# DVE alone for the operations that DVE or POOL could do, after the attention of a two-layer streaming encoder

## The chip, the core and the metric

The program runs on one core of one Trainium2 chip. The core has a matrix engine (TensorE, PE in the profile; its weight loads are shown as PEld), three engines for elementwise work (VectorE or DVE, ScalarE or ACT, GpSimd or POOL) and SyncE (SP), whose queue issues the DMAs here. Each engine works through its own list of instructions in order, and semaphores hold an instruction until its inputs are there and its output buffer is free. The metric is the device time of one execution in microseconds; lower is better.

## What is computed

The reference is one inference step of two layers over a prompt of 2048 tokens and a sample of 32 tokens, width 1024, float32 throughout. Layer 0 projects, attends in two head groups (a sliding window and a chunk band), multiplies each head group's output with its SiLU gate and projects back. Layer 1 is a gated linear recurrence. Cut to what bears on the change:

```python
# layer 0, after the two attentions (oa, ob) and their gates (ga, gb)
y = jnp.concatenate([oa.reshape(b, t, -1) * jax.nn.silu(ga),
                     ob.reshape(b, t, -1) * jax.nn.silu(gb)], axis=-1)
m = y @ w_out
x = x + rms_norm(m, ln_post[0])
...
# layer 1
xb, z = jnp.split(rms_norm(x, ln_pre[1]) @ w_in, 2, axis=-1)
xp = jnp.concatenate([conv_state, xb], axis=1)
xc = conv_b + xp[:, 0:t] * conv_w[0]
for tap in range(1, CONV_W):
    xc = xc + xp[:, tap:tap + t] * conv_w[tap]
...
r = jax.nn.sigmoid(blockdiag(xc, wa) + ba)
gi = jax.nn.sigmoid(blockdiag(xc, wx) + bx)
log_a = C_GATE * r * jax.nn.log_sigmoid(lam)
a = jnp.exp(log_a)
u = jnp.sqrt(-jnp.expm1(2.0 * log_a)) * (gi * xc)
_, hs = lax.associative_scan(_lin_combine, (a, u), axis=1)
m = (hs * jax.nn.silu(z)) @ w_out
x = x + rms_norm(m, ln_post[1])
```

## The kernel before

**Tiling.** Activations lie transposed, channels on the 128 partitions and tokens along the free axis. The 2084 token columns (2048, four of padding, 32) are six blocks of 352 columns (the last 324); two blocks make one of three groups `b`. A float32 product is made of three faster ones: each operand is split into a high part and a remainder (`h = copy(x)` in a rounded type, `l = x - h`), and PE adds `wh*xh`, `wh*xl` and `wl*xh`. So every weight tile (128 x 1024) and every activation that PE reads needs one cast (ACT or DVE) and one subtraction (DVE or POOL). In the profile `wst` is the weight as loaded, `wh` and `wl` its parts, `r0h`, `r0l`, `r1h`, `r1l` the two sets of split activations.

**Stages.** First layer 0's input projections beside the attention; then, from `dense_2`, layer 0's out projections for the three groups (`out_part`), the first of which runs before the attention is over; then for each group layer 1's input projection (`in_part`) and out projection (`out_part`).

- `y_proc` makes the input of layer 0's out projections: product of attention output and gate (`xt<-xt`, `ex<-ex`), cast on ACT, subtraction (`r1l`, `r0l`).
- `out_part` runs the matmuls; for each finished accumulator `fin_out` scales it into `m` on ACT, squares it and adds the square to `sacc`; after the last of eight, the norm's factor `r` is made, and for each half block `m` is multiplied by `r` (`m<-m,r`) and the residual is added (`m<-m,xr` or with another buffer's name), each in a piece of five and one of three rows of 176 columns (128x880 and 128x528).
- `norm_proc` normalizes the next input and splits it.
- `in_part` has, for each of eight channel blocks, a convolution on DVE (`ex<-xb`), a split for the gate matmuls (`xs`), activations on ACT (`e`, `ti`, `a`), the recurrence as a scan on DVE, and the split of the result into the out projection's operand. The buffers `e` and `ti` are named `eti` and `ti` in the profile, `xc`, `a` and `sz` are `ex`. `gw_proc` loads and splits the gate weights (`gst`, `gh`, `gl`).
- `w_split` casts and subtracts each new weight tile. Of layer 1, weights are split once in group 0, stored, and loaded ready-split in groups 1 and 2.

**The order.** The program is written out by a list scheduler, `Sched`, when the kernel is built. Each piece of work is a generator that yields a request `Req`: its engine or engines, its inputs, its buffers and, where there are several engines, a cost for each. The scheduler keeps a model of when each engine and tile is free; `run` goes through the waiting requests by rank, and `pick` chooses the engine. An engine may be taken only when its modelled end lies at most `LOOK` (0.6 us for DVE and POOL) ahead of the current time; among several, the one that ends first is taken. Ranks: 0 for `fin_out` and its additions, 0.4 for the convolution's chain, 0.5 for `y_proc`, 3 for `w_split`, which goes to 0.5 when no split weight is in hand. Requests that name DVE and POOL are those for `wl`, `r0l`/`r1l`, `xt<-xt`, `sacc`, `ss`, `m`, `xs`, `gl` and one product on `ti`. Others name DVE and ACT (the casts) or one engine alone. The loop over the engines of a request, with the line numbers of the profile's kernel:

```python
329        for i, e in enumerate(req.eng):
330            if e == "PE":
331                if t <= self.now + EPSR / 2:
332                    best = (0, e)
333                continue
334            if self.t[e] > self.now + LOOK[e] or t > max(self.now, self.t[e]) + EPSR:
335                continue
336            f = max(self.t[e], t) + (req.cost[i] if req.cost else 0.0) + (VPEN if e == "V" else 0.0)
```

All instructions go through the one helper at line 101, so the profile shows L101 for nearly every one of them; tiles are told apart by name.

Of the kernel before, what the change touches and what calls it, by code (L numbers as in the profile page):

```python
# [83 lines left out]
class Eng:  # L84


    def __init__(self, sch, name, eng):
        self.sch, self.name, self.eng = sch, name, eng
# [77 lines left out]
class Sched:  # L166
# [3 lines left out]
    def __init__(self):  # L170
        self.t = {"PE": 0.0, "A": 0.0, "V": 0.0, "G": 0.0, "SP": 0.0, "DMA": 0.0}
        self.w, self.r, self.key = {}, {}, {}
        self.procs = []
        self.now = 0.0
        self.n = 0
        self.tab = None
        self.lock = {"V": [], "G": []}
        self.win, self.busy, self.half = 0, 0.0, False
        self.pem, self.vpt = PEMA, VPTA
        self.halves, self.cuts, self.loaded = set(), {}, set()  # L180
# [100 lines left out]
    def set(self, key, t=None):  # L281
        self.key[key] = self.now if t is None else t

    def spawn(self, gen, prio):
        self.n += 1
        p = [prio, self.n, gen, None]
        p[3] = next(gen, None)
        if p[3] is not None:
            self.procs.append(p)
            self.procs.sort(key=lambda q: (q[0], q[1]))  # L290
# [30 lines left out]
    def pick(self, req):  # L321

        t = self.avail(req)
        if t is None:
            return None
        if req.eng[0] == "SP" and req.ins and not isinstance(req.ins[0], tuple):
            t += SPM
        best = None
        for i, e in enumerate(req.eng):
            if e == "PE":  # L330
                if t <= self.now + EPSR / 2:
                    best = (0, e)
                continue
            if self.t[e] > self.now + LOOK[e] or t > max(self.now, self.t[e]) + EPSR:
                continue
            f = max(self.t[e], t) + (req.cost[i] if req.cost else 0.0) + (VPEN if e == "V" else 0.0)
            if best is None or f < best[0]:
                best = (f, e)
        if best and req.func and self.tab and req.func != self.tab:

            if req.since is None:
                req.since = self.now
            if self.now < req.since + 1.0:
                return None
        return best and best[1]
# [49 lines left out]
def hybrid_kernel(ctx, tc, I, O):  # L395
    nc = tc.nc
    sch = Sched()
    V, A, G, PE, SP = [Eng(sch, n, e) for n, e in (("V", nc.vector), ("A", nc.scalar), ("G", nc.gpsimd),
                                                  ("PE", nc.tensor), ("SP", nc.sync))]
# [380 lines left out]
    def y_proc(b, ri, key, free=None, then=None):  # L780

        hh, hl = RT[ri]
        todo = [(bi, t0, col, w, 4 * j) for bi, t0, col, w in cells_of(b) for j in range(2)]
        cur = {}

        def y_load():
            for n, (_, t0, _, w, k0) in enumerate(todo):
                g = xrr if b == 0 and n % 3 == 2 else xtr
                x, = yield R("SP", [("o", min(b + 1, 2)), ("z", b)], [g])
                for j, src in enumerate((oT, zT)):  # L790
                    SP.dma_start(out=x[:, 4 * j:4 * j + 4, :w],
                                 in_=src[k0 * 128:k0 * 128 + 512, t0:t0 + w].rearrange("(k p) t -> p k t", p=128))
                cur[n] = x, g
                sch.set((key, "x", n))
        spawn(y_load(), PY if b == 0 else PY2)
        for n, (bi, t0, col, w, k0) in enumerate(todo):
            yield R("V", [(key, "x", n)])
            x, g = cur[n]
            o = x[:, 0:4, :w]
            e, _ = yield R(("V", "G"), [x], cost=(0.8, 1.63))  # L800
            ENG[e].tensor_tensor(o, o, x[:, 4:8, :w], OP.mult)
            ks, cs = slice(k0, k0 + 4), slice(col, col + w)
            yield R("A", [x] + ([(free, bi)] if free else []))
            A.copy(hh[:, ks, cs], o)
            th = sch.t["A"] + 0.13
            e, _ = yield R(("V", "G"), [lambda: th], cost=(0.8, 1.63))
            ENG[e].tensor_tensor(hl[:, ks, cs], o, f32(hh[:, ks, cs]), OP.subtract)
            g.release(x)
            if n % 4 == 3:
                sch.set((key, bi), max(sch.t["V"], sch.t["G"]) + 0.13)  # L810
        if then:
            then()
# [974 lines left out]
    def gw_proc():  # L1787

        for b in range(3):
            for c in range(8):  # L1790
                g, = yield R("SP", rings=[gstr])
                SP.dma_start(out=g, in_=I["gw"][c])
                e, (gh, gl) = yield R(("A", "V"), [g], [ghr, glr], cost=(0.3, 0.2))
                if e == "A":
                    A.copy(gh, g)
                else:
                    V.tensor_copy(gh, g)
                e, _ = yield R(("V", "G"), [gh], cost=(0.33, 0.69))
                ENG[e].tensor_tensor(gl, g, f32(gh), OP.subtract)
                gws[(b, c)] = gh, gl  # L1800
                gstr.release(g)
                sch.set(("gw", b, c), sch.t[e] + 0.13)
# [147 lines left out]
    def dense_2():  # L1950
        for b in range(3):
            yield from out_part(b, base + 8 * b, b % 2, I["xT"], LN_POST, x2T, lambda k, bi, b=b: (("y", b), bi), late_m=b > 0)
            if b == 0:

                yield R("PE", [("attention",)])
        spawn(gw_proc(), 1)
        xrr.retire(eti)
        for x in extra:
            xtr.retire(x)
        b1 = base + 24  # L1960
        for b in range(3):
            yield from in_part(b, b1 + 24 * b, 1, 0)
            if b < 2:
                spawn(norm_proc(x2T, b + 1, LN_PRE + 1, 1, (1, b + 1), [xtr, xtr], free=("in", b), src_ready=[("x2", b + 1)]), PY3)
            yield from out_part(b, b1 + 24 * b + 16, 0, x2T, LN_POST + 1, O["yT"], lambda k, bi, b=b: ("yc", b, k), late=True, final=b == 2)

    spawn(dense_2(), 9)
    sch.run(lambda: not names() & {"kq_proc", "v_proc", "proc", "reduce"})
    P.close()
# [25 lines left out]
    ar, szr = [Ring(sch, None, None, None, t, 1, tiles=[x]) for t, x in zip(("a", "sz"), parts[1])]  # L1995
    xtr.idle += [(0.0, -1, x) for x in extra]
    sch.set(("attention",))
    sch.pem, sch.vpt = PEM, VPT
    spawn(y_proc(1, 1, ("y", 1), then=y2), PY2)
    sch.run(lambda: not sch.procs)  # L2000
# [114 lines left out]
```

## Time and profile before

| what | us |
| --- | --- |
| median of three runs | 1881.93 |
| lowest and highest of them | 1880.21, 1882.59 |
| the profiled execution's own time | 1876.91 |
| its span in the profile | 1875.1 |

The profile is of one execution. Busy times are summed per engine and can lie beside each other; a matmul's time overlaps with the next one's. A row of a timeline gives start, duration, engine, line, operation, output and inputs with their shapes, and in brackets the idle time of the engine before it and what ended that. Where rows have "wait" in mind, as in "PE acc <- POOL wl", the engine on the left stood idle, and the instruction on the right was the one it waited for last. The stretches are in microseconds from the span's start.

### The profile page before, as it was taken

How to read it: one execution, taken by the hardware profiler on the slowest of the kernel's cores; microseconds unless marked ns; L12 is line 12 of the kernel's file. 1: busy time of each engine (PE TensorE's matmuls, PEld its weight loads, DVE VectorE, ACT ScalarE, POOL GpSimd, SP SyncE). 2: the span in 40 equal slices, each digit the busy share in tenths (PEclk: the TensorE clock that was granted, in tenths of full speed). 3: DMA queues.
4: the chain of work that ended last, by engine and by line, in shares of the span. 5: the costliest groups of instructions: out<-in, count | busy, mean ns of one | idle time of the engine just before them, and what ended most of it. 6: DMA issues, size and time to landing. Idle time of an engine off the chain costs nothing. (4 is left out here: it accounts for less than half of the span.)

```text
span 1875.1 us, 31799 instructions
## 1 busy us (share of the span) xinstructions
PE 1743.0 (93%) x11078; PEld 1686.8 (90%) x11078; DVE 1590.4 (85%) x3168; ACT 1002.5 (53%) x2048; POOL 610.6 (33%) x433
## 2 busy tenths in 40 slices
PE   8999999999999999999989969989889999999995
PEld 7999999889899999999979959988889999998995
DVE  8999967999999679989897879799898988699943
ACT  4276632476657337656564343456663586447831
POOL 4332214322223232221242646654423320153112
PEclk8999999999999999999999979999889999999997
DMA  5798856887554487877765884585455834565376
GB/s 177 205 252 262 233 151 211 228 249 211 168 157 119 128 237 186 245 202 203 212 190 153 225 231 134 191 258 175 154 174 186 238 121 149 182 200 167 128 269 177
DMA packets 293577, 362.80 MB, mean 193 GB/s; under 512 B 36309, under 2 KB 244617, under 8 KB 293401
## 3 DMA queue, kind: packets, MB, share of 16 engines
q1 hardware_dynamic: 293416, 360.78, 65.3%
q8 instruction: 87, 1.43, 0.3%
q14 instruction: 74, 0.60, 0.1%
HBM read 255.77 MB, written 107.00 MB: 193 GB/s over the span
## 5 line engine op out<-in xcount | busy, mean ns | idle before, releaser
L101 PE MATMUL acc<-r0h,wh 128*128 128x352 f32 (+2 forms) x1832 | 594.6, 325 | 16.3 <-ACT r0h L101 6.6
L101 PE MATMUL acc<-r0l,wh 128*128 128x352 f32 (+2 forms) x1832 | 595.1, 325 | 1.3 <-DVE r0l L101 1.3
L101 PE MATMUL acc<-r0h,wl 128*128 128x352 f32 (+2 forms) x1832 | 594.4, 324 | 1.5 <-DMA wl<-wo1s 1.5
L101 PEld LDWEIGHTS acc<-r0h,wh 128*128 128x128 f32 x1832 | 348.3, 190 | 19.4 <-ACT r0h L101 7.2
L101 PEld LDWEIGHTS acc<-r0l,wh 128*128 128x128 f32 x1832 | 348.2, 190 | 3.2 <-DVE r0l L101 2.2
L101 PEld LDWEIGHTS acc<-r0h,wl 128*128 128x128 f32 x1832 | 348.2, 190 | 3.2 <-DMA wl<-wo1s 2.5
L101 PE MATMUL acc<-r1h,wh 128*128 128x352 f32 (+1 forms) x864 | 282.8, 327 | 22.4 <-ACT xb L101 14.1
L101 PE MATMUL acc<-r1h,wl 128*128 128x352 f32 (+1 forms) x864 | 281.1, 325 | 15.2 <-POOL wl L101 15.2
L101 PE MATMUL acc<-r1l,wh 128*128 128x352 f32 (+1 forms) x864 | 281.0, 325 | 0.0
L101 POOL TENSOR_SCALAR pt<-pt,rr 128x256 f32<-128x256 f32 (+4 forms) x142 | 100.0, 715 | 366.2 <-DVE rr L101 214.3
L101 POOL TENSOR_TENSOR wl<-wst,wh 128x1024 fp32r<-128x1024 f32 x62 | 155.6, 2509 | 186.3 <-ACT wh L101 109.3
L101 ACT ACTIVATE pt<-pt,nm 128x256 f32<-128x256 f32 (+6 forms) x272 | 169.7, 626 | 61.2 <-DVE nm L101 59.3
L101 PEld LDWEIGHTS acc<-r1h,wh 128*128 128x128 f32 x864 | 166.1, 192 | 25.4 <-ACT xb L101 16.1
L101 PEld LDWEIGHTS acc<-r1h,wl 128*128 128x128 f32 x864 | 165.8, 192 | 15.5 <-POOL wl L101 15.5
L101 ACT CAST pp<-T 128x256 fp32r<-128x256 f32 (+4 forms) x314 | 134.0, 438 | 84.7 <-PE T L101 66.0
L101 PEld LDWEIGHTS acc<-r1l,wh 128*128 128x128 f32 x864 | 166.2, 192 | 0.0
L101 PE MATMUL T<-ident,pt 128*128 128x128 f32 (+2 forms) x864 | 143.4, 274 | 18.3 <-DVE pp L101 10.3
L101 DVE TENSOR_TENSOR pp<-T,pp 128x256 fp32r<-128x256 f32 (+4 forms) x314 | 150.4, 496 | 7.8 <-ACT pp L101 6.0
L101 PE MATMUL O<-pp,vt 128*128 128x256 f32 (+3 forms) x728 | 135.8, 309 | 10.0 <-DVE pp L101 4.7
L101 PEld LDWEIGHTS T<-ident,pt 128*128 128x128 f32 (+2 forms) x864 | 101.7, 140 | 42.7 <-DVE pp L101 19.9
L101 ACT CAST wh<-wst 128x1024 fp32r<-128x1024 f32 x70 | 73.5, 1049 | 99.7 <-PE acc L101 72.9
L101 PE MATMUL S<-kk,qa 128*128 128x320 f32 (+5 forms) x376 | 120.3, 334 | 3.6 <-issue 1.6
(252 smaller groups left out, 3312.8 us busy)
## 6 DMA issues: line engine op xcount, KB each, us to landing
wst<-w_in SPq DMA_DIRECT2D x93, 512.0 KB, 4.3
wst<-wo_in SPq DMA_DIRECT2D x32, 512.0 KB, 4.4
wh<-w1s SPq DMA_DIRECT2D x32, 512.0 KB, 3.7
wl<-w1s SPq DMA_DIRECT2D x32, 512.0 KB, 4.6
wh<-wo1s SPq DMA_DIRECT2D x24, 512.0 KB, 3.8
wl<-wo1s SPq DMA_DIRECT2D x24, 512.0 KB, 4.6
kk<-kB SPq DMA_DIRECT2D x32, 320.0 KB, 4.9
vt<-vB SPq DMA_DIRECT2D x16, 640.0 KB, 4.8
```

What stands on the lines that cost most here:

```text
L101: r = fn(*a, **k)
```

## The change

The scheduler gets a switch, `alone`. While it is on, `pick` passes over POOL for every request that names more than one engine; requests for POOL alone, and those for DVE and ACT, are as before. It is switched on when the attention's work is all placed, off after each input projection of layer 1 is placed, and on again ahead of the next one; after the last input projection it stays off. Nothing else is edited; the order of all later instructions is worked out anew by the scheduler.

```diff
@@ -175,6 +175,8 @@
         self.lock = {"V": [], "G": []}
+
+        self.alone = False
@@ -330,6 +332,8 @@
             if e == "PE":
                 if t <= self.now + EPSR / 2:
                     best = (0, e)
+                continue
+            if e == "G" and len(req.eng) > 1 and self.alone:
                 continue
@@ -1959,7 +1963,9 @@
         for b in range(3):
+            sch.alone = True
             yield from in_part(b, b1 + 24 * b, 1, 0)
+            sch.alone = False
             if b < 2:
                 spawn(norm_proc(x2T, b + 1, LN_PRE + 1, 1, (1, b + 1), [xtr, xtr], free=("in", b), src_ready=[("x2", b + 1)]), PY3)
@@ -1995,6 +2001,7 @@
     sch.set(("attention",))
+    sch.alone = True
     sch.pem, sch.vpt = PEM, VPT
```

## Prediction

> **What bounds the kernel now.** I read the page's busy times first, then TensorE's waits, then the busy time of each engine by stage, and last the timelines of DVE and POOL beside each other.
>
> ```profile
> span 1875.1 us, 31799 instructions
> PE 1743.0 (93%) x11078; PEld 1686.8 (90%) x11078; DVE 1590.4 (85%) x3168; ACT 1002.5 (53%) x2048; POOL 610.6 (33%) x433
> ```
>
> TensorE (PE) bounds the whole, but the share is a mean over stages. The windows cut the part that the change can touch into its stages; their columns are the stretch, its length, then busy time of PE, PEld, DVE, ACT and POOL, PE's granted clock, DMA share and GB/s.
>
> ```profile
> 1008.00:1206.00 198.00, 172.38 (x1051) 170.23 (x1050) 160.60 (x151) 75.59 (x136) 113.97 (x58) 0.94 0.71 204
> 1206.00:1364.00 158.00, 140.95 (x833) 138.90 (x832) 145.90 (x146) 97.00 (x128) 80.77 (x39) 0.95 0.60 200
> 1364.00:1442.00 78.00, 68.51 (x393) 66.72 (x392) 65.63 (x86) 38.60 (x60) 16.33 (x10) 0.91 0.53 180
> 1442.00:1586.00 144.00, 137.17 (x841) 135.38 (x840) 128.81 (x159) 94.83 (x124) 39.85 (x23) 0.99 0.52 160
> 1586.00:1649.00 63.00, 62.13 (x386) 61.35 (x385) 45.25 (x68) 28.12 (x50) 7.91 (x6) 1.00 0.59 189
> 1649.00:1786.00 137.00, 131.54 (x841) 129.54 (x840) 129.22 (x182) 96.28 (x155) 45.94 (x26) 1.00 0.55 166
> 1786.00:1875.00 89.00, 66.10 (x418) 63.86 (x416) 33.59 (x37) 19.33 (x41) 18.21 (x9) 0.89 0.74 228
> ```
>
> In order: the rest of layer 0's out projections, then layer 1's input and out projections in turn for the three token groups. The three input projections give PE nearly the same matmuls, and the first takes 158 us where the last takes 137. In the first DVE is busy 145.9 of 158 us. So the first two stages lose PE time, and DVE is full or nearly full. PE's waits over these stages (total, times, longest):
>
> ```profile
> PE acc L101 <- POOL wl L101: 15.2, 1, 15.2
> PE acc L101 <- ACT xb L101: 14.1, 6, 4.9
> PE acc L101 <- DVE ex L101: 8.3, 3, 4.7
> PE acc L101 <- ACT r0h L101: 6.6, 2, 5.7
> PE g L101 <- DVE xs L101: 6.4, 7, 1.6
> PE misc L101 <- DVE xs L101: 6.1, 2, 5.8
> PE acc L101 <- ACT tz L101: 3.2, 2, 2.2
> ```
>
> These seven come to 59.9 us, nearly all that can be won. `xb` on ACT waits for its one buffer, which DVE's convolution on `ex` frees, and `r0h` follows DVE's chain on `ti`; so most of the 59.9 us is DVE or POOL being late. Is DVE late by its own work? Its timeline beside POOL's:
>
> ```profile
> 1042.48 0.89 DVE L101 TENSOR_TENSOR r1l<-xt,r1h 128x704 fp32r<-128x704 f32 x1 [2.41 <-ACT r1h L101]
> ...
> 1046.27 3.14 DVE L101 TENSOR_TENSOR r1l<-xt,r1h 128x704 fp32r<-128x704 f32 x1 [0.24 <-ACT r1h L101]
> ```
>
> ```profile
> 1046.26 2.41 POOL L101 TENSOR_TENSOR wl<-wst,wh 128x1024 fp32r<-128x1024 f32 x1 [4.62 <-DVE wh L101]
> ```
>
> The same subtraction takes 0.89 us with POOL idle and 3.14 us when a POOL op of 2.41 us starts with it: 2.41 + 0.73. DVE stood still until POOL was done. The columns here are start, duration, engine, and the rest as named. A smaller tile even takes longer than a larger one:
>
> ```profile
> 1208.98 1.07 DVE L101 TENSOR_TENSOR m<-m,r 128x880 f32<-128x880 f32 x1
> ...
> 1211.52 2.59 DVE L101 TENSOR_TENSOR m<-m,r 128x528 f32<-128x528 f32 x1
> ```
>
> [...]
>
> **The change, part by part.** It adds no instruction, DMA or semaphore of its own; it takes POOL out of the choice for every request that names two engines, from the end of the attention on except while an out projection of layer 1 runs. The attention's last DVE op in the trace:
>
> ```profile
> 1007.96 0.42 DVE L101 TENSOR_TENSOR ot<-ot 64x256 f32<-64x256 f32 x1
> ```
>
> The first 1008 us are planned as before, and I count nothing there, nor in the two later out projections' own stretches or after 1786 us.
>
> *What goes onto DVE.* Prices of the same forms, first POOL's groups over all stages (count, busy us, mean ns), then DVE's ops with POOL idle:
>
> ```profile
> L101 POOL TENSOR_TENSOR wl<-wst,wh 128x1024 fp32r<-128x1024 f32 x24 | 63.2, 2634 | 62.1 <-ACT wh L101 30.1 <-DVE wh L101 15.7 <-PE g L101 9.0
> L101 POOL TENSOR_TENSOR xs<-ex,xs 64x704 fp32r<-64x704 f32 x12 | 25.7, 2140 | 18.1 <-DVE xs L101 10.3 <-ACT xs L101 7.6
> L101 POOL TENSOR_TENSOR m<-m,r 128x880 f32<-128x880 f32 x9 | 22.9, 2549 | 4.6 <-DVE r L101 4.3
> ```
>
> ```profile
> 1235.10 1.80 DVE L101 TENSOR_TENSOR xs<-ex,xs 64x704 fp32r<-64x704 f32 x2
> ...
> 1251.59 1.21 DVE L101 TENSOR_TENSOR wl<-wst,wh 128x1024 fp32r<-128x1024 f32 x1
> ```
>
> `wl` is 2.634 / 1.21 = 2.18, `xs` 2.140 / 0.90 = 2.38, `m` 2.549 / 1.07 = 2.38; I use 2.3. POOL's busy time in the four stages then costs DVE 113.97 / 2.3 = 49.6, 80.77 / 2.3 = 35.1, 39.85 / 2.3 = 17.3 and 45.94 / 2.3 = 20.0 us.
>
> *What goes from DVE.* I went through DVE's timeline of each stage, op by op, and took from each op the median of the same form with no POOL op beside it (for `m` 128x528, which never ran so, 0.67 us, an estimate scaled from the 1.07 us of 128x880). Ops over by more than 0.3 us were 38, 32, 19 and 22; first and last of each stage:
>
> ```profile
> 1014.39 1.64 DVE L101 TENSOR_TENSOR ex<-ex 128x704 f32<-128x704 f32 x1
> ...
> 1198.32 1.27 DVE L101 CAST wh<-wst 128x1024 fp32r<-128x1024 f32 x1 [3.44 <-PE acc L101]
> ...
> 1359.99 2.29 DVE L101 SCALAR_TENSOR_TENSOR ex<-xb,vec,ex 128x704 f32<-128x704 f32 x1
> ...
> 1442.62 2.41 DVE L101 TENSOR_TENSOR r1l<-xt,r1h 128x704 fp32r<-128x704 f32 x1
> ...
> 1575.67 1.43 DVE L101 TENSOR_TENSOR eti<-eti 128x704 f32<-128x704 f32 x1
> ...
> 1649.82 1.66 DVE L101 TENSOR_TENSOR xs<-sacc,xs 128x352 fp32r<-128x352 f32 x1
> ...
> 1777.13 2.32 DVE L101 SCALAR_TENSOR_TENSOR eti<-ex,eti 128x676 f32<-128x676 f32 x1
> ```
>
> (The second stage's first is the 2.59 us row above.) Their excess sums to 58.0, 46.9, 20.0 and 24.5 us. Net, DVE's load goes from 160.6 to 152.2, from 145.9 to 134.1, from 128.8 to 126.1 and from 129.2 to 124.7 us: 8.4 + 11.8 + 2.7 + 4.5 = 27.4 us less in all, though DVE does everything. In addition each moved op is ready in under half the time.
>
> *First stage, -8 us.* Its largest stall is one weight:
>
> ```profile
> 1090.57 0.66 PE L101 MATMUL acc<-r1h,wl 128*128 128x352 f32 x1 [15.21 <-POOL wl L101]
> ```
>
> ```profile
> 1055.00:1091.00 36.00, 20.52 (x125) 19.94 (x124) 31.73 (x19) 10.03 (x16) 29.48 (x14) 0.84 0.74 186
> ```
>
> In these 36 us POOL works 29.5 us ahead of and on that `wl`, and 17.2 us of DVE's 31.7 are such excess (same count). On DVE alone: 31.7 - 17.2 + 29.5 / 2.3 = 27.3 us, some 4.4 us less busy; with a part of the gaps between, 6 us off the 15.2. Next late is the 5.8 us wait for `xs` and the weight after it; with them -8, about the stage's net load.
>
> *First input projection, -9 us.* At 92% DVE sets the pace, so most of its 11.8 us should come back; I take three quarters, as the chain of PE, ACT and DVE of one column block has latency of its own.
>
> *Second and third, -2.5 and -2.5 us*: little PE time is lost there (144 and 137 us against 158).
>
> *The end of the first input projection, -2 us*: the 5.7 us wait for `r0h` follows DVE's last chain.
>
> Sum -24 us. The profiled execution took 1876.91 us (span 1875.1), so 1852.9 us; it lies 5.0 us under the median of the three runs, 1881.93, to which I apply the sum: **1858 us**.
>
> *Bounds.* If the excess stayed, each stage would take POOL's price less DVE's free time: 49.6 - 37.4, 35.1 - 12.1, 17.3 - 15.2 and 20.0 - 7.8, together +49.5 us. At the other end, all seven waits gone is -59.9 us. I stand nearer the second, since 3.14 = 2.41 + 0.73 is a row of this very stage.
>
> *Costed at nothing:* DVE's in-order queue. A `wl` or `gl` that had POOL to itself now stands among `m`, `xs` and the convolution, and whatever is behind it on DVE waits 0.4 to 1.2 us; SP's stores of `m` and PE's weights come behind that. It is covered as long as DVE's load stays under the stage; in the first input projection that cover is 158 - 134.1 = 24 us.
>
> **The rivals.**
>
> *Weights come late (slower).* The planner ranks weight splits last until no spare weight is in hand, and DVE is then the only engine for the subtraction. 24 `wl` were POOL's. If half of them were late by the running op (about 1), the own 1.2 us and the rest of a burst of `m` (about 1), that is 12 x 3.2 = 38 us; less the 17 us of the first two stages, and without the later 7, +21: 1903 us. It decides once `m`, `y` and the convolution alone keep DVE over about nine tenths. For it: 134.1 / 158 is 85% with bursts; against it: the worst weight now is late because of POOL.
>
> *DVE's order eats the gain.* Loads fall, but the new order puts other waits in place of the old ones: 0 to -9 us, about 1877 us. For it: the waits by `xb` and `xs` are the chain's, not POOL's alone.
>
> *DVE full.* [...] As a mechanism here: DVE's stretched time is real work, the price adds up, +49.5: 1931 us. The 0.89 and 3.14 us rows speak against it.
>
> *It does not do what it says*: the switch is set as the order is written, so the last `m` of an out projection may still be placed under the next input projection. That moves some 12 ops of 1 us, nothing that decides.
>
> **How the numbers follow.** The forecast (-10 to -46 us) 0.55, beyond that 0.03; eaten gain 0.20, half of it within 0.2%; late weights 0.17; DVE full 0.04; not as said 0.01, counted as no change. 0.2% is 3.8 us, about what a measurement can tell from no change. Faster 0.55 + 0.03 + 0.10 = 0.68, same 0.11, slower 0.21. The range 1836 to 1890 takes in the forecast, the eaten gain and the mild end of late weights.
>
> **What the next profile would show.** Right: POOL near zero from 1008 us but for the out projections; no `m` 128x528 on DVE over 0.8 us; the 15.2 us wait for `wl` under 10; the first input projection some 150 us. Wrong: PE waiting for DVE's `wl` again and again (late weights), or DVE above 97% with ops at their short durations (DVE full).

## The result and the profile after

| kernel | median us | lowest to highest |
| --- | --- | --- |
| before | 1882.26 | 1880.21 to 1882.73 |
| after | 1823.38 | 1822.28 to 1829.82 |

The ratio is 0.9696, with a 95% interval of 0.9673 to 0.972: 58.9 us less. The direction was right, and the size was not: 24 us were forecast, and the time lies below the range, which began at 1836. The profiled execution after took 1823.5 us, 53.4 us less than the one before, and its span is 53.4 us shorter too. The page of after:

```profile
span 1821.7 us, 31694 instructions
...
PE 1731.5 (95%) x11078; PEld 1671.8 (92%) x11078; DVE 1555.3 (85%) x3330; ACT 996.5 (55%) x2037; POOL 326.5 (18%) x284
```

DVE runs 162 instructions more than before and is busy 35.1 us less. PE's 11078 matmuls take 11.5 us less; the other 41.9 us of the span are idle time of PE that is gone. The windows of after, cut at the first matmul of each stage (columns as in the prediction: stretch, length, busy PE, PEld, DVE, ACT and POOL, granted clock, DMA share, GB/s):

```profile
1008.00:1183.30 175.30, 166.68 (x1039) 164.99 (x1038) 147.25 (x207) 76.70 (x135) 0.00 (x0) 0.99 0.80 233
1183.30:1327.60 144.30, 136.26 (x837) 132.82 (x836) 140.33 (x201) 101.85 (x131) 0.00 (x0) 1.00 0.59 202
1327.60:1393.30 65.70, 64.14 (x390) 63.52 (x390) 57.87 (x81) 30.42 (x50) 12.69 (x8) 0.97 0.69 238
1393.30:1537.00 143.70, 137.11 (x837) 133.24 (x836) 126.33 (x185) 92.24 (x120) 1.01 (x1) 1.00 0.52 160
1537.00:1600.50 63.50, 62.69 (x391) 61.90 (x390) 45.49 (x69) 28.45 (x50) 8.05 (x6) 1.00 0.58 188
1600.50:1735.50 135.00, 132.72 (x837) 130.06 (x837) 122.27 (x210) 93.80 (x152) 0.00 (x0) 1.00 0.54 168
1735.50:1821.70 86.20, 65.22 (x420) 62.61 (x418) 34.19 (x38) 19.47 (x41) 16.73 (x8) 0.92 0.73 236
```

POOL is at zero in the first and second stage and in the last input projection; its 1.0 us in the second input projection are the tail of an operation begun in the out projection. The granted clock of the first three stages rises from 0.94, 0.95 and 0.91 to 0.99, 1.00 and 0.97. Lengths by the same cut, in us ("same_order" is the first experiment below; L0 is the rest of layer 0's out projections, in and out are layer 1's projections of groups 0, 1, 2):

```
             L0    in0    out0   in1    out1   in2    last
before      198.0  157.3   78.8  143.4   63.7  136.6   89.3
after       175.3  144.3   65.7  143.7   63.5  135.0   86.2
difference  -22.7  -13.0  -13.1   +0.3   -0.2   -1.6   -3.1   sum -53.4
same_order  196.0  145.8   78.3  141.1   63.5  130.2   89.1   (sum -23.1 to before)
```

48.8 of the 53.4 us come from the first three stages. The cut at 1008 us also takes in what was won or lost earlier, where none of these three kernels is changed and PE's list is the same. The last matmuls of the attention show it (before, after, same_order):

```profile
1002.89 1.35 PE L101 MATMUL O<-pp,vt 128*128 128x256 f32 x10
...
1000.95 1.35 PE L101 MATMUL O<-pp,vt 128*128 128x256 f32 x10
...
1008.99 1.35 PE L101 MATMUL O<-pp,vt 128*128 128x256 f32 x10
```

So 1.9 us of the change's 53.4 lie ahead of it, and same_order comes 6.1 us late into its first stage; why single executions differ there isn't shown. Counted from these rows to the end of the span, the change gains 51.5 us and same_order 29.2. The rest of layer 0's out projections then takes 203.1 us before, 182.3 after and 195.0 in same_order.

PE's waits after, from 1000 us to the end (total, times, longest):

```profile
PE g L101 <- DVE xs L101: 11.0, 14, 2.8
PE acc L101 <- ACT tz L101: 3.6, 3, 2.1
PE acc L101 <- DMA wl<-wo1s: 2.9, 4, 1.1
PE acc L101 <- ACT tzb L101: 2.9, 1, 2.9
...
PE acc L101 <- DVE wl L101: 1.6, 1, 1.6
```

The 15.2 us for `wl`, the 14.1 for `xb` and the 6.6 for `r0h` are gone. What is left is short: no wait is over 2.9 us.

### The profile page after: what moved, and what is told of

The parts are those of the page before. It is cut to its first block, busy times and chain, and to the rows that moved or that the text cites. A ratio compares the mean times of both kernels' runs of the same rounds, so it can differ in the third digit from the quotient of the medians.

```text
span 1821.7 us, 31694 instructions
## 1 busy us (share of the span) xinstructions
PE 1731.5 (95%) x11078; PEld 1671.8 (92%) x11078; DVE 1555.3 (85%) x3330; ACT 996.5 (55%) x2037; POOL 326.5 (18%) x284
## 4 chain that ended last, share of the span: by engine, by line
PE 49%; DVE 29%; DMA 9%; ACT 6%; issue 4%; SPq 1%; POOL 1%; DVEq 0%; ACTq 0%; POOLq 0%
PE acc L101 35%; PE T L101 4%; PE O L101 4%; PE S L101 4%; DVE pt L101 3%; DVE ex L101 3%; DVE m L101 3%; DMA xr<-x2T 3%; DVE ss L101 2%; DVE ti L101 2%; DVE xs L101 2%; DVE s L101 2%; DVE pp L101 2%; DVE eti L101 1%; DVE wl L101 1%
## 5 line engine op out<-in xcount | busy, mean ns | idle before, releaser
L101 PE MATMUL acc<-r1h,wh 128*128 128x352 f32 (+1 forms) x864 | 277.5, 321 | 5.2 <-ACT tz L101 3.6
L101 PE MATMUL acc<-r1h,wl 128*128 128x352 f32 (+1 forms) x864 | 277.0, 321 | 1.6 <-DVE wl L101 1.6
L101 PE MATMUL acc<-r1l,wh 128*128 128x352 f32 (+1 forms) x864 | 276.9, 321 | 0.0
L101 PEld LDWEIGHTS acc<-r1h,wh 128*128 128x128 f32 x864 | 162.3, 188 | 6.4 <-ACT tz L101 4.5
L101 PEld LDWEIGHTS acc<-r1l,wh 128*128 128x128 f32 x864 | 162.3, 188 | 0.0
L101 DVE CUSTOM_DVE_ANT_0 pt<-S,bias 128x320 f32<-128x320 f32 (+2 forms) x240 | 108.8, 478 | 17.4 <-PE S L101 14.6
L101 PEld LDWEIGHTS O<-pp,vt 128*128 128x128 f32 (+1 forms) x728 | 107.1, 193 | 16.0 <-DVE pp L101 6.1
```

Source lines behind the costliest of these rows:

```text
L101: r = fn(*a, **k)
```

## The experiments

Two theories stand against each other. **Standstill**: the gain is DVE no longer stopping behind POOL, and the order of the instructions is a side effect. **Order**: with one fast engine in place of two, the scheduler writes another order for every engine (and shares the casts out anew between DVE and ACT), and that order is a gain of its own. Ratios are to the kernel before on the same chip, whose median lay between 1870.84 and 1877.28 us; intervals are of 95%.

### same_order: before's order, POOL's operations on DVE

The scheduler plans as before; each operation that it gives to POOL from the attention's end on, where the change would bar POOL, is written into DVE's list at that place. The lists of PE, ACT and SP stay as they were.

```diff
-        fn = getattr(self.eng, op)
+        fn = getattr(self.sch.dve if self.name == "G" and self.sch.alone else self.eng, op)
...
-            if e == "G" and len(req.eng) > 1 and self.alone:
-                continue
```

> The order of before kept for PE, ACT and SP, and 142 instructions moved from POOL into DVE's list where the planner had put them; nothing is planned anew. Theory P (DVE stands still while POOL works, and every queue that waits for either is late): most of the 58.9 us comes back without a new plan, 1825 to 1845 us, and the 15.2 us wait of PE for wl falls under 6. Rival O (the gain is the new order: the weight's cast moved ahead of the m block in ACT's list): the time stays at 1865 us or more, since ACT's list is that of before and the cast still stands behind the m block.

Measured: 1854.13 us against 1876.37, ratio 0.9873 (0.9843 to 0.9902): 22.2 us less of the 58.9, between the times that the two theories gave. By the traces 146 instructions have moved (POOL has 433 before and 287 here). The groups of DVE by form, from 1008 to 1790 us, show that the standstills are gone. First before, then same_order (count | busy us, mean ns | idle before):

```profile
L101 DVE TENSOR_TENSOR m<-m,r 128x528 f32<-128x528 f32 x9 | 23.1, 2569 | 0.0
...
L101 DVE COPY hist<-xb 128x3 f32<-128x3 f32 x24 | 10.0, 415 | 0.4
```

```profile
L101 DVE TENSOR_TENSOR m<-m,r 128x528 f32<-128x528 f32 x18 | 12.6, 700 | 0.0
...
L101 DVE COPY hist<-xb 128x3 f32<-128x3 f32 x24 | 3.9, 164 | 0.8 <-ACT xb L101 0.3
```

DVE does twice as many of these `m` in about half the time. The windows of same_order, its first three stages:

```profile
1008.00:1204.00 196.00, 177.58 (x1093) 175.59 (x1092) 152.28 (x213) 77.67 (x140) 0.94 (x1) 0.96 0.71 205
1204.00:1349.80 145.80, 135.83 (x828) 134.40 (x828) 132.17 (x185) 96.34 (x127) 0.00 (x0) 0.98 0.66 216
1349.80:1428.10 78.30, 67.84 (x398) 66.10 (x397) 65.69 (x86) 39.07 (x61) 15.17 (x10) 0.93 0.54 180
```

The first input projection has the gain, 11.5 us, and so has the first stage once it is counted from the attention's last matmuls, 8.1 us; the first out projection has nearly none. PE's waits, from 1008 to 1800 us:

```profile
PE acc L101 <- DVE wl L101: 9.3, 1, 9.3
PE misc L101 <- DVE xs L101: 9.1, 5, 5.3
PE acc L101 <- ACT r0h L101: 7.9, 2, 5.7
```

The longest wait falls from 15.2 to 9.3 us and stays at its place; the 5.7 us for `r0h` at the start of the first out projection do not move at all. So the standstills are worth 22 us under the old order by the medians, and 29 by the profiles from the attention's end; the rest of the 58.9 us is not theirs.

### l0_only and in_only: the switch in one part each

```diff
@@ l0_only, ahead of each in_part
-            sch.alone = True
+            sch.alone = False
@@ in_only, at the end of the attention
-    sch.alone = True
```

> DVE alone only from the end of the attention to the first input projection of layer 1; POOL is used again after that. Theory P: the first stage shortens by some 22 us as in the changed kernel (198 to 175 us) and the later stages stay as before: 1857 to 1862 us. Rival S (the stages are not independent, a good start of the input projection needs the first one too): under 1850 us.

> DVE alone only in the three input projections of layer 1; the rest of layer 0's out projections keeps POOL. Theory P: the first input projection and the out projection behind it shorten by 13 us each, the others by 2 or 3 together: 1850 to 1860 us, and with the other half this sums to the 58.9 us. If the first stage's gain carries the rest: over 1868 us.

Measured: l0_only 1857.0 us, ratio 0.9891 (0.986 to 0.9922); in_only 1867.86 us, 0.9945 (0.9928 to 0.9962). Their gains, 19.4 and 8.5 us, are 27.9 together, some half of what the whole gives. l0_only's first stage is 177.6 us, 2.3 longer than the change's; counted from the attention's last matmuls the two are alike (182.6 and 182.3 us). in_only gains in its first input and out projections (145.2 and 63.0 us) and loses it in the second input projection, at 161.6 us; there PE's waits show one large one:

```profile
PE acc L101 <- ACT r1h L101: 16.4, 1, 16.4
```

Nothing in POOL's absence explains a new wait of 16.4 us: each variant has an order of its own, and they do not add up. in_only's time lies in neither of the ranges given for it, just under the 1868 us of the rival.

### wl_only: POOL left out for the weights alone

```diff
-            if e == "G" and len(req.eng) > 1 and self.alone:
+            if e == "G" and len(req.eng) > 1 and self.alone and req.cost == (1.14, 2.3):
```

> Only the weights' subtraction wl leaves POOL, 24 of its groups' instructions, 63 of about 280 us of POOL time in the four stages; everything else may use POOL as before. If the gain is the weight that PE waited 15.2 us for: 1855 us or less. Theory P (each us of POOL costs DVE nearly as much, whatever the operation): about 63/280 of 58.9 us, so 1865 to 1872 us.

Measured: 1864.01 us, 0.9933 (0.9906 to 0.9959). This is the rival of late weights where it does occur:

```profile
PE acc L101 <- DVE wl L101: 35.9, 3, 17.1
```

With POOL still at `m`, `xs` and the rest, a weight on DVE queues behind operations that stand still. The timeline has it ahead of the two longest: at the 17.1 us a `sacc` takes 2.35 us (0.57 on average in same_order) and the weight itself 2.58 for 1.21, and at the 13.2 us four pieces of `xt` take 5.56 us together (0.52 each in same_order) beside POOL's `r1l`. In the changed kernel the same wait is 1.6 us.

### after_pool and no_lock: the new order with POOL in it, and a plan without the lock

after_pool keeps the lists of PE, ACT and SP of the changed kernel and gives every second of the operations concerned to POOL (163 were counted ahead of the run; the traces have 166, POOL going from 284 to 450). no_lock lets POOL in, and takes out the scheduler's model of DVE and POOL shutting each other out (`book` moves an operation behind a running one of the other engine where all operands lie in SBUF).

```diff
@@ after_pool, where every second request of a cost sets ghost
-        fn = getattr(self.eng, op)
+        fn = getattr(self.sch.gps if self.name == "V" and self.sch.ghost else self.eng, op)
@@ no_lock, in book (the skip in pick goes too, and so does the switching off)
-        if e in ("V", "G") and op not in ("reciprocal", "tensor_reduce") and all(str(x.space).endswith("SB") for x in outs + ins):
+        if not self.alone and e in ("V", "G") and op not in ("reciprocal", "tensor_reduce") and all(str(x.space).endswith("SB") for x in outs + ins):
```

> The other half of the cross: the changed kernel's order for PE, ACT and SP kept to the instruction, and every second instruction that the change had taken from POOL, or DVE had before, put back on POOL (163 of them). In the order of before, POOL's work cost about 24 us (ratio 0.9873 without it). Theory B (two separate gains, the stalls of DVE and the new order): the order's gain stays, the stalls return: 1840 to 1860 us against 1823 of the changed kernel. Rival (the order only works with DVE alone, since its waits were placed for short operations): 1880 us or more, no better than before.

> POOL may be chosen everywhere, as before; only the planner's own model from the end of the attention on no longer counts DVE and POOL as shutting each other out. If before's poor order came from that model alone (it makes chains late on paper): an order like the changed kernel's, under 1860 us. If the model only tells what the chip does: the plan gets too early for the chip, and the time is 1876 us or more.

Measured: after_pool 1891.67 us, 1.0067 (1.0041 to 1.0093); no_lock 1912.09 us, 1.0175 (1.0146 to 1.0205). The first two stages and the second and third input projections of after_pool:

```profile
1008.00:1204.40 196.40, 176.70 (x1050) 173.28 (x1049) 146.27 (x136) 77.44 (x137) 134.41 (x72) 0.95 0.72 210
1204.40:1366.40 162.00, 139.38 (x836) 135.58 (x835) 151.23 (x162) 101.86 (x131) 77.95 (x36) 0.97 0.54 179
...
1434.80:1589.00 154.20, 139.63 (x838) 136.45 (x837) 130.72 (x156) 92.53 (x121) 52.72 (x31) 0.98 0.48 149
...
1652.50:1798.20 145.70, 136.20 (x838) 133.37 (x837) 123.93 (x181) 93.23 (x151) 48.96 (x28) 0.98 0.51 156
```

DVE has 71 instructions fewer than after in the first stage (136 against 207) and is busy as long (146.3 against 147.3 us); in the first input projection it has 39 fewer and is busy 10.9 us longer. In these two stages POOL's help takes 1.0 us of busy time from DVE and adds 10.9. So the new order is no gain by itself either: with POOL in it, it is slower than before. POOL's part is dealt out by count there and not chosen by the scheduler; a better share was not tried. And the scheduler's lock is worth having: without it the time is the worst of all.

### to_end and from_start: POOL left out in more places

```diff
@@ to_end, after each in_part
-            sch.alone = False
@@ from_start, the same and in __init__
-        self.alone = False
+        self.alone = True
```

> POOL is left out to the end, in layer 1's out projections too. There POOL works 8 to 18 us in each stage and PE waits for little but DMA: within 4 us of the changed kernel, 1820 to 1828 us. If DVE is short of time at the end (m and the residual of the last group): 1828 to 1835 us.

> POOL is left out from the first instruction, for everything that DVE could do as well. In the first 1008 us POOL is busy 288 us and DVE 881 us. If the shared stops cost as much there: under 1815 us. If POOL's work there is of one input or beside PSUM work, and DVE (87% busy) becomes the bound: 1840 us or more.

Measured: to_end 1837.79 us, 0.9772 (0.9735 to 0.9808); from_start 1847.03 us, 0.9832 (0.9803 to 0.9861). Both are faster than before, and to_end's time is above both ranges given for it. from_start is slower than the change; to_end is slower than the change's first measurement (0.9696), while its interval overlaps that of the second (0.9717 to 0.9767, below). In from_start PE reads layer 0's `r1` of the second group first at 1051.22 us, before at 1050.55: in the first 1008 us DVE takes over POOL's 287.6 us of work and is busy only 28.1 us longer (909.5 for 881.4), and still nothing is won, in an order that is another there too. Nor does every operation of DVE stand still there: before, at 563.37 us, a `pt<-S,bias` of 128x320, whose `S` lies in PSUM, takes 0.48 us in the middle of a POOL `wl` (562.22 us, 2.41 long), and the group's 192 take 482 ns on average. So POOL's absence does not pay everywhere. The out projections of layer 1, the only part that to_end newly takes from POOL, stay as long as after (66.0 and 63.4 us); what grows is the second input projection, to 153.0 us. Again the place is not where the edit is.

### order_pool, order_dve, gates_early: single features of the new order

The new order differs from before's at two places where PE stood still. Weights are split earlier; and the last gate matmuls of the first input projection stand ahead of the out projection. Before, the out projection's first matmul comes at 1363.28 us, and the last gate matmul after it:

```profile
1363.28 0.32 PE L101 MATMUL acc<-r0h,wh 128*128 128x352 f32 x1
...
1367.01 0.32 PE L101 MATMUL g<-xs,gl 128*128 128x352 f32 x1
1367.17 0.32 PE L101 MATMUL acc<-r0l,wh 128*128 128x352 f32 x1
1367.33 0.32 PE L101 MATMUL acc<-r0h,wl 128*128 128x352 f32 x1
1373.35 0.66 PE L101 MATMUL acc<-r0h,wh 128*128 128x352 f32 x1 [5.70 <-ACT r0h L101]
```

The gate's results feed the recurrence whose last part is that `r0h`: they stand 23 matmuls late in the list, and a wait of 5.7 us follows. That the one causes the other is a conjecture, which gates_early puts to the test. After, the last gate matmul comes at 1315.29 us, and the out projection's first is the 77th behind it:

```profile
1315.29 0.32 PE L101 MATMUL g<-xs,gl 128*128 128x352 f32 x1
...
1327.57 0.32 PE L101 MATMUL acc<-r0h,wh 128*128 128x352 f32 x1
```

order_pool makes a weight urgent while one is still in hand, with POOL; order_dve is the same lists with POOL's part on DVE; gates_early raises the rank of the last copies into `xb` in same_order, which puts the last gate matmuls 25 ahead of the out projection's first.

```diff
@@ order_pool and order_dve
-        sch.reprio("w_split", PW if wcur[1] - 1 - wcur[0] >= WAHEAD else PWU)
+        sch.reprio("w_split", PW if wcur[1] - 1 - wcur[0] >= (1 if ("attention",) in sch.key else WAHEAD) else PWU)
@@ gates_early
-PX, PXL, PXN = 0.4, 0.4, 6
+PX, PXL, PXN = 0.4, -0.5, 6
```

> The kernel before with POOL as free as it was; only the weight splits get their urgent rank one weight earlier after the attention. That puts the cast of the late weight ahead of the m block in ACT's list, and the last gate matmuls of the first input projection 57 matmuls ahead of the out projection's first one, where before had them 23 behind it. Theory Q (the two large stalls of PE, 15.2 us for wl and the slow start of the first out projection, are these two places in the lists, and POOL is not needed to explain them): the first out projection of layer 1 takes some 66 us in place of 79, the wait for wl falls under 6 us, and the whole is 1855 to 1865 us. If only DVE alone can remove them: 1875 us or more.

> The same lists for PE, ACT and SP as in the run named order_pool, and POOL's instructions put into DVE's list in the changed kernel's stretches. Theory Q: the order's gain and the gain of DVE alone in the order of before (24 us) add up: 1830 to 1842 us. If DVE alone is only worth that much with lists planned for it: within 10 us of order_pool.

> The run named same_order with one rank changed: the convolution chain of the last two channel blocks goes ahead of the other work. The last gate matmuls of the first input projection then stand 25 matmuls ahead of the out projection's first one (same_order: 23 behind). The first 200 us are as in same_order. Theory Q: the first out projection falls from 78 us to 64 to 70, the rest stays, 1840 to 1848 us. If the place of the gates is not the cause: 1850 us or more.

Measured: order_pool 1876.09 us against 1870.84, 1.0021 (1.0003 to 1.0039); order_dve 1848.29, 0.9879 (0.9861 to 0.9898); gates_early 1847.72, 0.9878 (0.9855 to 0.99). In order_pool the wait for `wl` is gone from the list, and these stand in its place:

```profile
PE acc L101 <- POOL r1l L101: 11.5, 1, 11.5
PE g L101 <- DVE xs L101: 11.2, 9, 2.8
PE acc L101 <- ACT r1h L101: 9.4, 1, 9.4
```

gates_early shortens the first out projection from 78.3 to 72.3 us, but its first input projection takes 156.6 where same_order's took 145.8, and the wait of 5.7 us for `r0h` is still in the out projection, at 1371.2 us. order_dve's time lies in neither of the ranges given for it. Neither feature carries the gain; the idea that one such place was the cause falls. With order_pool and order_dve a pair on one chip again gives the price of POOL under one order: 27.8 us.

### rank, after_again, hybrid, hybrid2: how much an order can be worth

The scheduler has a clock of its own while it writes the kernel. Its length, from the first matmul that reads `r1` in layer 0's second out projection to the first of layer 1's last out projection, can be set beside the same stretch of each trace:

```
              planned   measured   over the plan (us)
before          684.7      735.2       50.5
same_order      684.7      706.2       21.5
after           662.3      686.9       24.6
l0_only         681.2      708.7       27.5
in_only         686.7      725.3       38.6
wl_only         686.6      722.3       35.7
to_end          677.1      697.9       20.8
from_start      685.0      705.6       20.6
order_pool      694.9      736.9       42.0
order_dve       694.9      702.2        7.3
gates_early     689.1      705.1       16.0
after_pool      662.3      747.9       85.6
no_lock         653.5      764.4      110.9
```

Where DVE works alone in the change's stretches, the chip is 7 to 25 us over the plan; where POOL works beside it, in some parts or in all, 28 to 111. The last column is not one measure for all rows: the plans of same_order, order_dve and gates_early still book POOL's operations, that of after_pool books none of those it deals out, and that of no_lock leaves the standstills out. By that table the change has two halves: 25.9 us that were over the plan (50.5 to 24.6), and 22.4 us by a plan that is shorter (684.7 to 662.3). The measured column has them as 29.0 us for the engine under the old order (735.2 to 706.2) and 19.3 for the new order with DVE alone (706.2 to 686.9). If the plan tells what an order is worth, a change of rank that only lengthens the plan must cost what the plan says. rank keeps POOL out exactly as the change does and alters one rank:

```diff
-PX, PXL, PXN = 0.4, 0.4, 6
+PX, PXL, PXN = 0.6, 0.4, 6
```

Its plan is 686.5 us, 24.2 longer than the change's. after_again is the changed kernel, not edited. hybrid and hybrid2 are the change up to the second and third input projection; the later ones are planned with POOL, and POOL's part is written into DVE's list (the flag `moved` does in them what same_order's edit does):

```diff
-            sch.alone = True
+            sch.alone, sch.moved = b < 1, b >= 1
@@ hybrid2
-            sch.alone = True
+            sch.alone, sch.moved = b < 2, b >= 2
```

> The changed kernel up to the first out projection of layer 1; in the second and third input projection the planner may choose POOL again, but what it gives to POOL is put into DVE's list. In same_order these two stages took 141.1 and 130.2 us, in the changed kernel 143.7 and 135.0. If that holds behind the changed kernel's start as well: 1815 to 1820 us, under both kernels. If the two stages depend on what stands before them: 1822 us or more.

> The changed kernel with one rank of the planner shifted (the convolution chain of the first six channel blocks from 0.4 to 0.6). DVE is as alone as in the changed kernel, and does the same instructions; only the lists differ. By the planner's own clock the stretch from the last third of layer 0's out projections to the last out projection of layer 1 is 686.5 us long, where the changed kernel has 662.3 and the kernel before 684.7, and all of the 24 us lie in the second input projection (158.1 for 134.5). Theory L (time = the planned length + an overrun of 20 to 28 us with DVE alone, 40 to 50 with POOL sharing, so that about half of the 59 us is a shorter plan): 22 to 26 us slower than the changed kernel run beside it, about 1845 us, the second input projection near 165 us. If the gain is DVE's alone and the lists only follow: within 6 us of the changed kernel.

> The changed kernel up to the third input projection; in that one alone, what the planner gives to POOL is put into DVE's list. Planned length 662.9 us against 662.3. In the run named hybrid that stage took 130.0 us, in the changed kernel 135.0. Theory L with that stage's overrun of 1 us in place of 6: 3 to 6 us under the changed kernel. If the tail gives it back (90.9 us in the run named hybrid, 86.2 in the changed kernel): the same within 2 us.

> The changed kernel, unedited, on the chip of the two others, as their measure: ratio to the kernel before 0.967 to 0.972 by its first measurement; the two theories say the same.

Measured: rank 1849.77 us, 0.9851 (0.9837 to 0.9866), and after_again 1827.57 us, 0.9742 (0.9717 to 0.9767), on the same chip (the same kernel gave 0.9696 on another): 22.2 us from one rank, with POOL doing the same operations; a few casts change sides with the order (of those into `r0h` from `eti`, DVE has 4 where it had 10). The wait is in rank's second input projection, and it is the one that in_only had, where the two plans are also long (158.1 and 157.8 us for that stage, against 134.5 in the change's):

```profile
PE acc L101 <- ACT r1h L101: 16.4, 1, 16.4
```

By the scheduler's clock and the trace rank stands at 686.5 planned and 707.8 measured, 21.3 over the plan, as the others without POOL. So an order can be worth as much as the standstills, and here the plan foresees it.

For the change itself the plan foresees it only in part. By the scheduler's clock the new order shortens the rest of layer 0's out projections by 2.4 us, the first input projection by 7.9 (145.5 to 137.6) and the first out projection by 10.9 (73.0 to 62.1). From same_order to after the profiles have 12.7, 1.5 and 12.6 us less there, and 2.6 and 4.8 more in the two later input projections. The first out projection is the plan's; the first stage's 12.7 us are not, and that the totals of 22.4 and 19.3 lie so near is in part chance. In that first stage the waits of 9.3 us for `wl` and 5.3 for `xs` that same_order keeps are gone.

hybrid took 1823.66 us, 0.9747 (0.9726 to 0.9768), and hybrid2 1823.14, 0.9705 (0.9685 to 0.9726). hybrid2 is 4.4 us under after_again on its chip, its third input projection 130.7 against 134.4 us; the intervals overlap, so that it beats the changed kernel isn't settled.

## Why the prediction was wrong in size

**The mechanism was right.** DVE stood still behind POOL (`m` 128x528 took 2.57 us on average before and 0.70 in same_order), and DVE alone is busy for less. The loads forecast for DVE, 152.2, 134.1, 126.1 and 124.7 us, came out at 147.3, 140.3, 126.3 and 122.3. The estimate of 0.67 us for `m` 128x528 is 0.70 in same_order (its row above). The 15.2 us wait was to lose 6: under the old order it lost 5.9.

**The step that failed is the sum**, together with "the first 1008 us are planned as before, and I count nothing there", whose other side was never drawn: what comes later is planned anew, and I counted there only what the loads and waits of the old order would become. For that order the sum is good: -24 forecast, -22.2 us by same_order's medians, -29.2 in its profile from the attention's end. What it leaves out is the new order, another 22.3 us in the profiles by the same count. The order appeared in the prediction only as a danger (the rival "DVE's order eats the gain", 0 to -9 us), never as a gain, so the range had no room for it below.

**By terms.** Counted from the attention's last matmuls, the first stage was put at -8 and gave -20.8; the first out projection, in the -2 us for the end of the first input projection, gave -13.1. These two are the mis-sized terms, and the excess is the order's: in same_order they gave -8.1 and -0.5. The -2 stood on the 5.7 us wait for `r0h`, and that wait did not move there. The first input projection was put at -9 and gave -13.0, in same_order -11.5. The second and third were put at -2.5 each and gave +0.3 and -1.6, in same_order -2.3 and -6.4. So under the old order every term but one comes within 2.5 us of what was measured, and the third input projection gave 3.9 us more than its term. To read a stage's gain off DVE's net load holds that far, and only while the order stays.

**The bound of -59.9** held all seven waits. In the profile after, waits of these names still come to 17.4 us, so 42.5 of the 59.9 are gone. It was not a bound on the whole, though: 11.5 us of the gain are PE's busy time, and the waits did not contain them. After the 5.7 us wait PE ran on at a granted clock of 0.50 for 6.7 us (last section), so that wait cost more than its own length.

**The rivals.** Late weights are real, and worst with POOL beside DVE (35.9 us in wl_only); with DVE alone the wait is 9.3 us under the old order and 1.6 after. "DVE full" said +49.5. One of its signs came: DVE is busy 140.3 of 144.3 us, 97%, in the first input projection, with short operations (the 16 `wl` there take 1.22 us on average). But that stage is 13 us shorter than before, so a full DVE was no reason to keep POOL: after_pool, with 166 operations given to POOL, is 3 to 4% slower than the changed kernel.

**Open.** Why the shorter plan arises is not shown as a rule: rank jumps by 24 us for a step of 0.2, so some of it is the luck of a list. Why the new order is worth 12.7 us in the first stage, where the plan has 2.4, is not shown beyond the waits that are gone. Why the third input projection is 5 us shorter under before's order than after is not explained. What in the chip makes DVE stop behind POOL is not shown; the rows show that it does. Whether all of POOL's operations stop DVE alike, those with one input too, wasn't tried.

## What to carry to other kernels

Before giving POOL a share of DVE's work, compare the same DVE operation with and without a POOL operation beside it: here `r1l` took 0.89 us with POOL idle and 3.14 beside a POOL operation of 2.41, and the two engines were 27.8 us slower than DVE alone under one order (order_pool against order_dve). Where a scheduler writes the order, a change in what an engine may do is two changes, the durations and a new order; keep the old order and swap only the engine to price the first, and read the scheduler's own clock for the second, stage by stage. The two need not add: here the new order gained only with DVE alone. And compare profiles from a point that the change cannot reach; 6 us of drift ahead of it can pass for a stage's missing gain. A gain in one part under an order of its own need not be there when the parts are put together.

## What the hardware showed beside

**A small copy stands still too.** A copy of 128 x 3 elements takes 0.16 us (the group of same_order above); before, beside POOL's `wl`, it took 2.37. The timeline of before, DVE and POOL:

```profile
1347.35 0.89 DVE L101 SCALAR_TENSOR_TENSOR e<-ex,e 128x704 f32<-128x704 f32 x1
...
1347.57 2.92 POOL L101 TENSOR_TENSOR wl<-wst,wh 128x1024 fp32r<-128x1024 f32 x1 [8.95 <-PE g L101]
...
1348.15 2.37 DVE L101 COPY hist<-xb 128x3 f32<-128x3 f32 x1
```

The copy ends at 1350.52, 0.03 us after POOL's operation (1347.57 + 2.92 = 1350.49): it stood until POOL was done.

**After the 5.7 us wait the clock was 0.50.** The windows of before around this wait, which is for `r0h`:

```profile
1367.50:1373.30 5.80, 0.15 (x1) 0.00 (x0) 4.50 (x6) 5.64 (x9) 1.35 (x1) 0.71 0.67 224
1373.30:1376.00 2.70, 2.39 (x7) 2.01 (x8) 2.67 (x3) 2.67 (x3) 0.00 (x0) 0.50 0.44 173
1376.00:1380.00 4.00, 4.00 (x15) 4.00 (x14) 3.87 (x5) 0.88 (x2) 0.00 (x0) 0.50 0.00 0
```

From 1373.3 to 1380 us the granted clock is 0.50. Its matmuls in the timeline:

```profile
1376.20 0.49 PE L101 MATMUL acc<-r0l,wh 128*128 128x352 f32 x1
...
1376.49 0.49 PE L101 MATMUL acc<-r0h,wl 128*128 128x352 f32 x1
```

They start every 0.29 us, where those at 1367.17 and 1367.33 were 0.16 apart. That is some 20 matmuls with 0.13 us extra, about 2.6 us on top of a wait of 5.7 (an estimate from these rows). The half rate lasted 6.7 us here from PE's first matmul after the wait; from 1380.24 us on a matmul of this form takes 0.32 us again, and the next ones start at 1380.40 and 1380.57.
